# A buffer of its own for x, both halves per k-step, ten matmuls on zeros ahead of all, and later statistics in a decoder trunk on one NeuronCore

## The chip, the cores and the metric

The kernel runs on one core of a Trainium2 chip (trn2). The metric is the device time of one execution in microseconds (us). The profile is one execution, recorded by the hardware profiler. PE stands for TensorE's matmuls, PEld for its weight loads, DVE for VectorE, ACT for ScalarE, POOL for GpSimd, SP for SyncE, whose queue issues the large loads.

## What is computed

The reference is a small decoder trunk on 256 tokens of 1024 float32 channels. Two layers; each is a half-step FFN, a token mixer and another half-step FFN, each behind its own RMS norm:

```python
def rmsnorm(x, g):
    y = x * rsqrt(mean(x * x, axis=-1, keepdims=True) + 1e-6)
    return y * g

def swiglu_half_step(h, g, w1, w3, w2):
    u = rmsnorm(h, g)
    return h + 0.5 * ((silu(u @ w1) * (u @ w3)) @ w2)

h = x
h = swiglu_half_step(h, ...)                  # layer 0, FFN 0
h = h + mamba2_mixer(rmsnorm(h, ssm_norm), ...)
h = swiglu_half_step(h, ...)                  # layer 0, FFN 1
k_shared, v_shared = shared_kv(h, ...)
h = swiglu_half_step(h, ...)                  # layer 1, FFN 0
h = h + sliding_window_attention(rmsnorm(h, attn_norm), k_shared, v_shared, ...)
h = swiglu_half_step(h, ...)                  # layer 1, FFN 1
```

w1 and w3 are 1024 x 2816, w2 is 2816 x 1024. All of it is float32, and the weights are read once.

## The kernel before, in words

**Precision.** Each float32 operand is split into two parts of a faster type (float32r): a high part, made on ScalarE by a cast, and the remainder, made on VectorE by a subtraction. A product is then three matmuls (`wmm3`, L136): high x high, high x low, low x high. Almost all matmuls have 128 x 128 weights and 256 moving columns (the 256 tokens).

**Weights.** `Unit` (L142) takes a 1 MB piece of weights: a tile `raw` (three buffers, pool `rawp`), loaded by SyncE (L151), and for each 512 columns a cast `wh` on ScalarE (L164) and a subtraction `wl` on VectorE (L165). High and low parts have eight half-size buffers each, that is, four units. `up_unit` (L176) holds four of the eight k-tiles of 256 columns of w1 and w3; `row_unit` (L189) holds 256 rows of w2.

**FFN.** `run_ffn` (L294) goes through eleven chunks c of 256 hidden channels. For each chunk and each half f of 128 channels, `up(c, f)` (L330) makes w1's and w3's products in one PSUM bank `pm`: 2 x 8 k-tiles x 3 = 48 matmuls. `gate` (L315) makes silu(a) * b and splits it into `ghl`; `flush` (L363) adds the down product of a gated half into four PSUM banks `acc`: 24 matmuls. The first half of the first chunk runs k-tile by k-tile, with w1 and w3 in turn; all other halves run w1 over all k-tiles and then w3.

**The norm.** The up products of the first two chunks don't wait for the RMS norm: they use the hidden state times the gain, split into `vh` and `vl` (L242), and `gate` multiplies by the tokens' scale afterwards (L318). The later chunks use the normalized `uTh`, `uTl`, made by `normalize` (L282). The scale is made in steps: `square` (L249) squares the hidden state on ScalarE and adds the four parts on GpSimd (L255, L257); `stats` (L267) takes the mean with four small matmul instructions (`pc`), then VectorE and GpSimd make the reciprocal root `rs`; `scale` (L279) spreads it over partitions with matmuls (`pb`) and copies it to `rsb` (L222). When `stats` and `scale` are put into TensorE's stream is said by `at`: after so many matmuls of this FFN (`later`, L123, and `tick`, L126). It is (114, 134) for the first FFN and (60, 84) for the others. Where the second number is above 96 (`slow`, L392), the gates of chunk 0 and the normalize are put behind the third group of up products, not behind the second; in that case the first three flushes (72 down matmuls) follow the fourth group.

**The start.** x (1 MB) is loaded in two halves into `xin`, which takes one of the three raw buffers (L58); two weight units take the other two. `turn_x(b)` (L1110) transposes two of the eight k-tiles of x on TensorE, splits them into `vh`, `vl`, and splits the part of the weights that goes with them. b = 0 and 1 run ahead of the first FFN; 2 and 3 run inside the first half's k loop, at k = 3 and 5 (`pre`, L1135). `keep_x` (L1126), at k = 7, copies the transposed x from PSUM to `hT` on VectorE (L1129) and starts the squares. `gain_cols` (L198) transposes the gains.

**PSUM.** Three pools: `ps_mm` with two banks, `ps_acc` with four, `ps_tr` with two. The first half's `pm` is in `ps_acc`, the others are in `ps_mm`; the last two transposed pieces of x take two banks of `ps_acc`, and the four `acc` banks come from there as well.

**The order of work.** The framework orders each engine's instructions when the program is built: by the program's order as priority, and by a model of when inputs and buffers come free. Each engine then runs its list strictly in order. So matmuls of the second half may stand among those of the first, and a small load of a later stage may stand early in GpSimd's list: mamba's first tiles (L449 to L492) are filled in the first 10 us.

Of the kernel before, what the change touches and what calls it, by code (L numbers as in the profile page):

```python
# [11 lines left out]
F32 = mybir.dt.float32  # L12
# [6 lines left out]
P = 128  # L19
D = 1024  # L20
KT = D // P
S = 256
NT = S // P
# [17 lines left out]
def yoco_kernel(ctx: ExitStack, tc: tile.TileContext, a: dict, out: bass.AP):  # L41
    nc = tc.nc
# [3 lines left out]
    rawp = ctx.enter_context(tc.tile_pool(name="rawp", bufs=3))  # L46
# [3 lines left out]
    ps_mm = ctx.enter_context(tc.tile_pool(name="ps_mm", bufs=2, space=PSUM))  # L50
    ps_acc = ctx.enter_context(tc.tile_pool(name="ps_acc", bufs=4, space=PSUM))
# [3 lines left out]
        return bass.AP(tensor=src.tensor, offset=src.offset + off, ap=[[0, parts], [1, n]])  # L55

    x2 = a["x"][0]
    xin = rawp.tile([P, NT, D], F32, tag="raw", name="xin")  # L58
    xsrc = x2.rearrange("(t p) c -> p t c", p=P)
    nc.sync.dma_start(xin[:, :, 0:512], xsrc[:, :, 0:512])  # L60
    grow = [sb.tile([4 * KT, P], F32, tag="g", name="grow0", bufs=3),
# [23 lines left out]
    uTh = const.tile([P, KT, S], F32R, name="uTh")  # L85
    uTl = const.tile([P, KT, S], F32R, name="uTl")
# [3 lines left out]
    def nm(s):  # L90
        uid[0] += 1
        return f"{s}_{uid[0]}"
# [102 lines left out]

    gcols = []

    def gain_cols(g):  # L198
        n = g.shape[0]
        pg = ps_mm.tile([P, n], F32, tag="mm", name=nm("pg"))  # L200
        nc.tensor.transpose(pg, g, ident[:n, :n])
        gc = const.tile([P, n], F32, name=nm("gcol"))
        nc.scalar.copy(gc, pg)
        gcols.append(gc)
# [89 lines left out]
    def run_ffn(layer, j, cur, nxt, hook=None, ups=None, at=(60, 84), pre=None):  # L294
# [4 lines left out]
        ups = {} if ups is None else ups  # L299
# [15 lines left out]
        def gate(c, pm):  # L315
            if c < 2:
                t = sb.tile([P, 512], F32, tag="cv", name=nm("tp"), bufs=2)
                nc.vector.tensor_mul(half(t), half(pm), two(cur.rb))  # L318
                pm = t
            sl = sb.tile([P, 256], F32, tag="g", name=nm("sl"), bufs=3)  # L320
            nc.scalar.activation(sl, pm[:, 0:256], AF.Silu)  # L321
            g = sb.tile([P, 256], F32, tag="g", name=nm("g"), bufs=3)
            nc.vector.tensor_mul(g, pm[:, 256:512], sl)  # L323
            ghl = sb.tile([P, 512], F32R, tag="ghl", name=nm("ghl"), bufs=4)
            gh, gl = ghl[:, 0:256], ghl[:, 256:512]
            nc.scalar.copy(gh, g)
            nc.vector.tensor_sub(gl, g, gh.bitcast(F32))
            return gh, gl

        def up(c, f):  # L330
            u = units(c)
            xh, xl = (cur.vh, cur.vl) if c < 2 else (uTh, uTl)
            pool, tag = (ps_acc, "acc") if c == 0 and f == 0 else (ps_mm, "mm")
            pm = pool.tile([P, 512], F32, tag=tag, name=nm("pm"))

            def one(k, w, first, stop):
                wh, wl = u[k // 4].get((k % 4) * 512 + w * 256 + f * P, P)
                wmm3(pm[:, w * 256:(w + 1) * 256], wh, wl, xh[:, k, :], xl[:, k, :], first, stop)

            if c == 0 and f == 0:  # L340
                for k in range(KT):
                    if pre and k in pre:
                        pre[k]()
                    for w in range(2):
                        one(k, w, k == 0 and w == 0, k == KT - 1 and w == 1)
            else:
                for w in range(2):
                    for k in range(KT):
                        one(k, w, k == 0, k == KT - 1)
            return pm  # L350

        def down(c, f, d, g):
# [29 lines left out]

        pend = []

        def start_gates(pm):
            if hook is not None:
                cur.keep_eps()
            pend.append((0, 0, gate(0, g00)))
            pend.append((0, 1, gate(0, pm)))
            cur.normalize()  # L390

        slow = at[1] > 96  # L392
        for c in range(NCHUNK):
            for f in range(2):
                if c == 0 and f == 0:
                    later(*stats)
                    later(*scale)
                    with tc.issue_after(pe[-1]) if pe else nullcontext():
                        g00 = up(c, f)
                    continue  # L400
                pm = up(c, f)
                if c == 0 and not slow:
                    start_gates(pm)
                if c == 0:
                    g01 = pm
                    continue
                if slow and c == 1 and f == 0:
                    start_gates(g01)
# [493 lines left out]
    def attention(ap, cur, kT, vtok, bias, nxt):  # L902
# [199 lines left out]
    n0 = norms[0]  # L1102
    n0.open()
    w13 = a["ffn_w1"][0, 0], a["ffn_w3"][0, 0]
    ups = {0: [up_unit(*w13, 0, 0, 2, True,
                       lambda: nc.sync.dma_start(xin[:, :, 512:1024], xsrc[:, :, 512:1024]))]}
    ups[0].append(up_unit(*w13, 0, 1, 2, True))
# [18 lines left out]
    def keep_x():  # L1126
        for b, px in enumerate(pxs):
# [55 lines left out]
```

## Time and profile before

| what | value |
|---|---|
| median of 3 runs | 1079.51 us (1075.5 to 1083.77) |
| the profiled execution's own time | 1079.0 us |
| its span, first to last instruction | 1077.3 us |
| mean granted TensorE clock | 0.989 |
| loads from memory | 187.00 MB, 175 GB/s over the span |

The first FFN takes the stretch from the start to 206 us, mamba that to 413, the second FFN that to 604, the third that to 780; attention ends at 882 and the last FFN at the end.

How to read the rows: a row of a timeline has start, duration, engine, line, operation, what is written from what, shapes, count, and in brackets the engine's idle time before it and what ended that. A row of the chain of waits has start, duration, what. In a table of windows each engine has its busy time and, in brackets, the number of its instructions; then come the granted TensorE clock (1.00 is full), the mean share of the DMA engines and GB/s. A matmul's duration in a row is its latency; matmuls overlap, so what one costs is the distance from start to start.

### The profile page before, as it was taken

What the parts mean: (1) busy time and instruction counts of PE and PEld (TensorE: products, weight loads), DVE (VectorE), ACT (ScalarE), POOL (GpSimd) and SP (SyncE); (2) the same over time, 40 slices, a digit from 0 to 9 for tenths busy, and PEclk for the clock granted to TensorE, in tenths of its full rate; (3) what the DMA queues carried; (4) which work ended last, traced back from release to release, by engine and by line L of the source; (5) the groups of instructions that cost most, each with busy time, mean ns of one, the idle gap of its engine ahead of it and who ended that gap; (6) DMA issues with size and microseconds to landing.
All of it is one profiled execution on the core that took longest, in us unless ns stands there. A gap on an engine that the chain in (4) does not pass through costs nothing.

```text
span 1077.3 us, 20452 instructions
## 1 busy us (share of the span) xinstructions
PE 1049.3 (97%) x8262; PEld 1009.5 (94%) x8262; DVE 697.8 (65%) x1383; ACT 580.9 (54%) x1200; POOL 108.7 (10%) x104
## 2 busy tenths in 40 slices
PE   7999999999989989999999999999999999999998
PEld 6999999999879989999999999999997699999997
DVE  6955546784898877754555976555576769454543
ACT  5644545666876846553454755444565656353541
POOL 4000000103415123000000200010012010000000
PEclk9999999999989989999999999999999999999999
DMA  7566456548567345564656465665552326564641
GB/s 246 193 224 208 159 195 192 161 157 229 145 206 244 118 119 160 195 198 163 226 157 196 157 196 183 207 237 196 172 182 79 118 79 201 190 210 143 205 148 40
DMA packets 140944, 189.45 MB, mean 176 GB/s; under 512 B 4893, under 2 KB 120785, under 8 KB 140849
## 3 DMA queue, kind: packets, MB, share of 16 engines
q1 hardware_dynamic: 139632, 185.62, 53.4%
q0 software_dynamic: 1168, 2.51, 0.9%
q8 instruction: 65, 1.06, 0.4%
q14 instruction: 31, 0.25, 0.1%
q10 hardware_dynamic: 48, 0.02, 0.0%
HBM read 187.00 MB, written 1.12 MB: 175 GB/s over the span
## 4 chain that ended last, share of the span: by engine, by line
PE 85%; DVE 6%; ACT 3%; DMA 2%; issue 2%; POOL 1%; SPq 0%; ACTq 0%; DVEq 0%; POOLq 0%
PE pm L103 44%; PE acc L103 22%; PE pp L103 6%; PE pa L103 5%; PE pq L101 2%; DVE wl L165 2%; PE pa L101 1%; DMA raw<-in_ssm_w_in_dram 1%; POOL sq L255 1%; PE pz L103 1%; ACT wh L164 1%; DVE y L757 1%; PE ps L101 1%; PE po L101 1%; DVE sp L953 1%
## 5 line engine op out<-in xcount | busy, mean ns | idle before, releaser
L165 DVE TENSOR_TENSOR wl<-raw,wh 128x512 fp32r<-128x512 f32 x676 | 445.7, 707 | 148.9 <-ACT wh L164 147.7
L164 ACT CAST wh<-raw 128x512 fp32r<-128x512 f32 x676 | 378.8, 618 | 201.3 <-PE pm L103 100.7
L103 PE MATMUL pm<-uTh,wh 128*128 128x256 f32 x1152 | 323.4, 281 | 0.0
L103 PE MATMUL pm<-uTl,wh 128*128 128x256 f32 x1152 | 323.4, 281 | 0.0
L103 PE MATMUL pm<-uTh,wl 128*128 128x256 f32 x1152 | 323.3, 281 | 0.0
L103 PEld LDWEIGHTS pm<-uTh,wh 128*128 128x128 f32 x1152 | 217.2, 189 | 0.9 <-issue 0.2
L103 PEld LDWEIGHTS pm<-uTl,wh 128*128 128x128 f32 x1152 | 216.9, 188 | 0.6
L103 PEld LDWEIGHTS pm<-uTh,wl 128*128 128x128 f32 x1152 | 217.2, 189 | 0.0
L103 PE MATMUL acc<-ghl,wh 128*128 128x256 f32 x1056 | 190.6, 282 | 0.0
L103 PEld LDWEIGHTS acc<-ghl,wh 128*128 128x128 f32 x1056 | 162.3, 188 | 0.0
L103 PE MATMUL acc<-ghl,wl 128*128 128x256 f32 x528 | 148.8, 282 | 0.0
L323 DVE TENSOR_TENSOR g<-pm,sl 128x256 f32<-128x256 f32 x72 | 30.3, 421 | 135.8 <-ACT sl L321 135.8
L321 ACT ACTIVATE sl<-pm 128x256 f32<-128x256 f32 x72 | 27.3, 380 | 165.2 <-PE pm L103 165.2
L103 PEld LDWEIGHTS acc<-ghl,wl 128*128 128x128 f32 x528 | 99.5, 188 | 0.0
L103 PE MATMUL pp<-uTh,wl 128*128 128x256 f32 x288 | 82.9, 289 | 4.6 <-DVE wl L165 4.6
L103 PE MATMUL pp<-uTh,wh 128*128 128x256 f32 x288 | 83.4, 291 | 1.4 <-ACT uTh L291 1.4
L103 PE MATMUL pp<-uTl,wh 128*128 128x256 f32 x288 | 83.1, 290 | 0.2 <-DVE uTl L292 0.2
L255 POOL TENSOR_TENSOR sq<-sq,sq 128x512 f32<-128x512 f32 x18 | 27.8, 1544 | 519.0 <-ACT sq L251 519.0
L103 PE MATMUL pm<-vh,wl 128*128 128x256 f32 x256 | 74.3, 291 | 2.1 <-DVE wl L165 2.1
L103 PE MATMUL pm<-vh,wh 128*128 128x256 f32 x256 | 74.7, 292 | 0.5 <-DVE tp L318 0.3
L103 PE MATMUL pm<-vl,wh 128*128 128x256 f32 x256 | 73.9, 289 | 0.8 <-DVE vl L244 0.8
L103 PEld LDWEIGHTS pp<-uTh,wl 128*128 128x128 f32 x288 | 56.5, 196 | 4.8 <-DVE wl L165 4.8
(235 smaller groups left out, 1502.1 us busy)
## 6 DMA issues: line engine op xcount, KB each, us to landing
raw<-in_ffn_w_dram SPq DMA_DIRECT2D x172, 512.0 KB, 4.9
raw<-in_ffn_w_dram SPq DMA_DIRECT2D x44, 1024.0 KB, 5.3
raw<-in_ssm_w_in_dram SPq DMA_DIRECT2D x16, 1024.0 KB, 5.4
raw<-in_ssm_w_out_dram SPq DMA_DIRECT2D x8, 1024.0 KB, 4.9
em<-pdram SPq DMA_DIRECT2D x8, 768.0 KB, 11.0
raw<-in_ssm_w_in_dram SPq DMA_DIRECT2D x8, 512.0 KB, 4.8
raw<-in_w_q_dram SPq DMA_DIRECT2D x4, 1024.0 KB, 4.9
raw<-in_w_o_dram SPq DMA_DIRECT2D x4, 1024.0 KB, 5.0
```

Of the source, the lines that this page charges most:

```text
L101: r = op(*args, **kw)
L103: r = op(*args, **kw)
L164: return (nc.scalar.copy(wh, rs).ins, nc.vector.tensor_sub(wl, rs, wh.bitcast(F32)).ins)
L165: nc.vector.tensor_sub(wl, rs, wh.bitcast(F32)).ins)
L255: nc.gpsimd.tensor_add(self.sq, self.sq, sq)
L321: nc.scalar.activation(sl, pm[:, 0:256], AF.Silu)
L323: nc.vector.tensor_mul(g, pm[:, 256:512], sl)
L757: nc.vector.scalar_tensor_tensor(out=y2, in0=zs[:, j, :], scalar=gn(ct), in1=rb, op0=ALU.mult, op1=ALU.mult)
L953: chain[1] = op(*args, **kw).ins
```

## The change

- `xin` comes from a pool of its own, `xp`, with a 128 x 128 tile of zeros, `dummy`. The pool is closed behind the first FFN, so that mamba's pool takes over its memory.
- `keep_warm(10)` puts ten float32 matmuls of `dummy` by `dummy` (into a `ps_mm` bank that nobody reads) ahead of all other work of TensorE.
- `up_first` takes the place of the two halves of chunk 0, in all four FFNs: for each k-tile, both halves, and in each w1 and w3, so 12 matmuls per k-tile. In the first FFN both `pm` banks are in `ps_acc`.
- In the first FFN the third group, `up(1, 0)`, also runs k-tile by k-tile.
- In the first FFN `turn_x(2)`, `turn_x(3)` and `keep_x` run at k = 2, 4 and 7 of this longer loop, and `at` is (122, 143).
- In the second FFN (layer 0, FFN 1) `at` is (72, 95); in the other two it stays (60, 84).

```diff
     x2 = a["x"][0]
-    xin = rawp.tile([P, NT, D], F32, tag="raw", name="xin")
+    xpool = ExitStack()
+    xp = xpool.enter_context(tc.tile_pool(name="xp", bufs=1))
+    xin = xp.tile([P, NT, D], F32, name="xin")
+    dummy = xp.tile([P, P], F32, name="dummy")
+    nc.vector.memset(dummy, 0.0)
...
+    def keep_warm(n):
+        pw = ps_mm.tile([P, P], F32, tag="mm", name=nm("pw"))
+        for i in range(n):
+            nc.tensor.matmul(pw, dummy, dummy, start=True, stop=True)
+
...
+        def up_one(c, f, pm, k, w, first, stop):
+            xh, xl = (cur.vh, cur.vl) if c < 2 else (uTh, uTl)
+            wh, wl = units(c)[k // 4].get((k % 4) * 512 + w * 256 + f * P, P)
+            wmm3(pm[:, w * 256:(w + 1) * 256], wh, wl, xh[:, k, :], xl[:, k, :], first, stop)
+
+        def up_first():
+            pms = [ps_acc.tile([P, 512], F32, tag="acc", name=nm("pm")),
+                   (ps_acc if pre else ps_mm).tile([P, 512], F32, tag="acc" if pre else "mm", name=nm("pm"))]
+            for k in range(KT):
+                if pre and k in pre:
+                    pre[k]()
+                for f in range(2):
+                    for w in range(2):
+                        up_one(0, f, pms[f], k, w, k == 0 and w == 0, k == KT - 1 and w == 1)
+            return pms
+
         def up(c, f):
...
+            pm = ps_mm.tile([P, 512], F32, tag="mm", name=nm("pm"))
+            if c == 1 and f == 0 and pre:
                 for k in range(KT):
-                    if pre and k in pre:
-                        pre[k]()
                     for w in range(2):
-                        one(k, w, k == 0 and w == 0, k == KT - 1 and w == 1)
-            else:
-                for w in range(2):
-                    for k in range(KT):
-                        one(k, w, k == 0, k == KT - 1)
+                        up_one(c, f, pm, k, w, k == 0 and w == 0, k == KT - 1 and w == 1)
+                return pm
+            for w in range(2):
+                for k in range(KT):
+                    up_one(c, f, pm, k, w, k == 0, k == KT - 1)
             return pm
...
-        def start_gates(pm):
+        def start_gates():
             if hook is not None:
                 cur.keep_eps()
-            pend.append((0, 0, gate(0, g00)))
-            pend.append((0, 1, gate(0, pm)))
+            for f in range(2):
+                pend.append((0, f, gate(0, g0[f])))
             cur.normalize()
...
+    keep_warm(10)
...
-    run_ffn(0, 0, norms[0], norms[1], ups=ups, at=(114, 134),
-            pre={3: lambda: turn_x(2), 5: lambda: turn_x(3), 7: keep_x})
+    run_ffn(0, 0, norms[0], norms[1], ups=ups, at=(122, 143),
+            pre={2: lambda: turn_x(2), 4: lambda: turn_x(3), 7: keep_x})
+    xpool.close()
...
-        run_ffn(0, 1, norms[2], norms[3])
+        run_ffn(0, 1, norms[2], norms[3], at=(72, 95))
```

More of the change, by code (lines that the diff above doesn't have):

```diff
@@ L328, in gate @@
             return gh, gl
-        def up(c, f):
[L331 to L340, printed above, removed]
+        def up_one(c, f, pm, k, w, first, stop):
[12 more added lines that the diff above has]
+            return pms
+        def up(c, f):
+            pm = ps_mm.tile([P, 512], F32, tag="mm", name=nm("pm"))
+            if c == 1 and f == 0 and pre:
                 for k in range(KT):
-                    if pre and k in pre:
-                        pre[k]()
                     for w in range(2):
-                        one(k, w, k == 0 and w == 0, k == KT - 1 and w == 1)
-            else:
-                for w in range(2):
-                    for k in range(KT):
-                        one(k, w, k == 0, k == KT - 1)
+                        up_one(c, f, pm, k, w, k == 0 and w == 0, k == KT - 1 and w == 1)
[3 more added lines that the diff above has]
+                    up_one(c, f, pm, k, w, k == 0, k == KT - 1)
             return pm
@@ L398, in run_ffn @@
                     with tc.issue_after(pe[-1]) if pe else nullcontext():
-                        g00 = up(c, f)
+                        g0 = up_first()
+                    if not slow:
+                        start_gates()
+                if c == 0:
                     continue
                 pm = up(c, f)
[L402 to L406, printed above, removed]
                 if slow and c == 1 and f == 0:
-                    start_gates(g01)
+                    start_gates()
                 g = gate(c, pm)
```

## The prediction

> **What bounds the kernel now.** I read the page's busy shares first, then what TensorE waits for, then the chain of waits from the start to 50 us, then the timelines of TensorE, VectorE and GpSimd at the places where TensorE stood.
>
> ```profile
> PE 1049.3 (97%) x8262; PEld 1009.5 (94%) x8262; DVE 697.8 (65%) x1383; ACT 580.9 (54%) x1200; POOL 108.7 (10%) x104
> ```
>
> TensorE is busy 97% of a span of 1077.3 us. The change takes no matrix product out, so it can only win where TensorE stands still or runs slowly. TensorE's waits:
>
> ```profile
> PE px L1115 <- DMA xin<-in_x_dram: 5.5, 2, 5.3
> ...
> PE pm L103 <- DVE wl L165: 2.1, 2, 1.1
> PE pc L103 <- POOL sq L257: 1.9, 2, 1.7
> ```
>
> The columns are us in total, times, longest. All three are in the up-projections that the change touches (pc is the token mean of `stats`). The windows of the start (us, engines' busy time, granted clock, DMA share, GB/s) and single matmuls:
>
> ```profile
> 7.80:12.40 4.60, 4.28 (x19) 3.99 (x20) 3.33 (x8) 3.21 (x9) 1.61 (x3) 1.00 1.09 345
> 12.40:24.10 11.70, 11.70 (x98) 11.63 (x97) 10.22 (x17) 7.70 (x16) 2.16 (x2) 1.00 0.81 269
> 24.10:28.70 4.60, 2.26 (x13) 1.47 (x13) 4.54 (x5) 3.97 (x9) 3.28 (x3) 1.00 0.46 163
> ```
>
> ```profile
> 29.48:32.90 3.42, 3.42 (x18) 3.42 (x18) 2.35 (x4) 1.67 (x3) 1.11 (x1) 0.51 0.69 199
> ```
>
> ```profile
> 11.54 0.42 PE L103 MATMUL pm<-vl,wh 128*128 128x256 f32 x1
> 11.75 0.42 PE L103 MATMUL pm<-vh,wl 128*128 128x256 f32 x1
> ...
> 13.13 0.28 PE L103 MATMUL pm<-vh,wl 128*128 128x256 f32 x1
> 13.25 0.28 PE L103 MATMUL pm<-vh,wh 128*128 128x256 f32 x1
> ...
> 32.24 0.96 PE L103 MATMUL pb<-ident,rs 128*128 128x128 f32 x4
> 32.94 0.37 PE L103 MATMUL pm<-vh,wh 128*128 128x256 f32 x1
> ```
>
> Until about 12.4 us a matmul follows the last after 0.21 us, later after 0.12: a half-speed start, though the clock column still says 1.00 there. TensorE stands for half of 24.1 to 28.7, and soon after, from 29.48 to 32.90, the granted clock is 0.51. Why it stands is in the chain of waits:
>
> ```profile
> 14.20 5.16 DMA raw<-in_ffn_w_dram
> ...
> 19.96 1.16 ACT sq L251 x2
> ...
> 21.20 1.30 POOL sq L255
> ...
> 27.14 1.07 POOL sq L257
> ...
> 28.25 0.61 PE pc L103 x4
> ...
> 41.05 8.62 PE acc L103 x72
> ```
>
> The third weight unit starts loading at 14.20, once x has left the raw buffer; ScalarE's in-order queue holds a cast of it, with the squares behind it; the squares feed GpSimd's adds; the adds feed pc. VectorE in the same time:
>
> ```profile
> 7.36 0.48 DVE L244 SCALAR_TENSOR_TENSOR vl<-px,gcol,vh 128x256 fp32r<-128x256 f32 x1 [7.36 <-ACT vh L243]
> ...
> 17.11 2.48 DVE L1129 COPY hT<-px 128x512 f32<-128x512 f32 x4
> 20.09 0.69 DVE L165 TENSOR_TENSOR wl<-raw,wh 128x512 fp32r<-128x512 f32 x1 [0.51 <-ACT wh L164]
> 21.65 7.70 DVE L165 TENSOR_TENSOR wl<-raw,wh 128x512 fp32r<-128x512 f32 x7 [0.87 <-ACT wh L164]
> ...
> 29.34 2.48 DVE L165 TENSOR_TENSOR wl<-raw,wh 128x512 fp32r<-128x512 f32 x4
> 33.23 0.42 DVE L222 COPY rsb<-pb 128x256 f32<-128x256 f32 x1 [1.41 <-PE pb L103]
> ...
> 46.41 0.42 DVE L327 TENSOR_TENSOR ghl<-g,ghl 128x256 fp32r<-128x256 f32 x1
> ```
>
> From 17 us VectorE has almost no idle time: 0.51, 0.87 and 1.41 us. Seven splits of weights took 7.70, where four took 2.48 (0.62 each, so seven are 4.3): 3.4 us were lost while GpSimd added. So two engines bound the start together, and TensorE's idle time is not all to be won.
>
> **The change, part by part, at the start.** *x in its own pool.* No load is added; the third unit (1 MB) waits for no buffer and follows the second one directly. At 345 GB/s (the first window) 1 MB is 3.0 us, so it has landed by about 15.5, before ScalarE is through with the second unit, and the idle 0.51 and 0.87 on VectorE go. The squares no longer stand behind a cast without data: the first can run after the first copy (17.11 + 0.68), at 17.8 instead of 19.96. Then pc can come at 26.1 instead of 28.25. Eighteen matmuls lie between `stats` and `scale`, before and after (both marks move by 8 or 9): 2.2 us at full speed, so pb is through by 28.7 and rsb can start at 29.4, 3.8 us sooner. VectorE allows less: its splits of the third and fourth unit end at 29.35 - 1.38 = 27.97, four of the next unit (2.48) stand in the same queue, so rsb starts at 30.45, 2.8 us sooner. What follows rsb is VectorE's: from 33.23 to 46.83 (gates of chunk 0, normalize, gate of (1,0)) it ran 13.6 us with hardly a pause, and the third group of down matmuls (24 of the 72 in the acc row, from 46.6) needs that gate. I carry the 13.6 over unchanged. **The start so wins 2.8 to 3.8; I take 3.3.** Above that the next thing late would be this VectorE chain, which TensorE would reach 2 to 3 us early, however the matmuls before it are arranged.
>
> *The memory behind x.* mamba's pool takes over x's place after the pool closes, so mamba's early small loads must now wait for the last transpose of x:
>
> ```profile
> 4.05 0.21 POOL L450 MEMSET rows<- 128x128 f32 x1
> ...
> 8.49 0.92 POOL L490 DMA_DIRECT2D wdt<-in_ssm_w_in_dram  x1
> ```
>
> ```profile
> 34.47 0.27 PE L463 MATMUL ptc<-ident,rows 128*128 128x128 f32 x1
> ```
>
> These 5.4 us of GpSimd's in-order queue move from 4.05-9.41 to about 14.0-19.4 (the load at 14.20 waited for the same transposes). The adds, behind them in time, could begin at about 19.0 (two squares after 17.8): cost 0.4 at most if the queue is as said, up to 1.0 if an add is put behind a load that waits. TensorE reads the first of the small tiles only at 34.47. I take 0.
>
> *Both halves per k-step; the second chunk in k order too.* Instructions and count stay (192 matmuls to the first flush). Each unit is asked for half as fast (12 matmuls, 1.43 us, per k, against VectorE's about 1.0 for a split of x and one of weights). From 12.4 to 24.1 TensorE was already continuously busy, because the framework put the second half's matmuls in between; so at the start: 0. The second half's accumulator moves to the other PSUM pool, so the fourth up group no longer waits for a gate; it sits under the VectorE chain: 0.
>
> *Ten matmuls on zeros.* They need only a VectorE fill, and VectorE is idle until 7.36. An f32 matmul is two instructions; two of them (four instructions) took 32.94 - 32.24 = 0.70 at low clock, so ten take 3.5 us, from about 1.2 to 4.7, and x comes at 5.27 (the 5.3 of the wait): hidden. If they start 1 us later they cost 0.5. What they may win: the 15 or so projections of 7.9 to 12.4 at 0.12 instead of 0.21, 1.4 us of TensorE. But the projections are fed by VectorE's splits, and VectorE sets the pace all the way to 46.83: bounds 0 and 1.0; I take 0, being nearer to the engine that is full. The Trainium skill ("TensorE: Matmul & The Clock Gate", Part 1) says the clock is judged in free-running windows of 3.4 us and falls back after an idle one, which speaks against the ten: behind them comes a thin stretch of transposes. The trace agrees so far as the clock was 0.51 for 3.4 us behind the thin stretch before 28.7; by the rule the warm clock may be gone again by 9 us and the ten win nothing, by the row of the cold matmuls they could win the 1.0.
>
> **The later FFNs.** The second FFN also takes its statistics later (72 instead of 60, 95 instead of 84):
>
> ```profile
> 413.18 0.28 PE L103 MATMUL pm<-vh,wh 128*128 128x256 f32 x1
> ...
> 422.24 0.61 PE L103 MATMUL pc<-mean,sq 128*128 128x1 f32 x4 [1.72 <-POOL sq L257]
> ...
> 433.30 0.41 PE L103 MATMUL acc<-ghl,wh 128*128 128x256 f32 x2
> ```
>
> ```profile
> 416.79 4.59 POOL L255 TENSOR_TENSOR sq<-sq,sq 128x512 f32<-128x512 f32 x1 [2.69 <-ACT sq L251]
> 421.46 0.72 POOL L257 TENSOR_TENSOR sq<-sq 128x256 f32<-128x256 f32 x1
> ```
>
> ```profile
> 417.17 3.09 DVE L165 TENSOR_TENSOR wl<-raw,wh 128x512 fp32r<-128x512 f32 x5
> ...
> 431.76 0.42 DVE L327 TENSOR_TENSOR ghl<-g,ghl 128x256 fp32r<-128x256 f32 x1
> ```
>
> Twelve more matmuls before pc are 1.44 us of cover for a wait of 1.72: pc would be asked for at 413.18 + 72 x 0.12 = 421.8 and the adds end at 422.18. **Win 1.4.** The price could be at the first flush: the gate was ready at 432.18, 1.1 before 433.30, and pb comes 9 to 11 matmuls (1.1 to 1.3 us) nearer to it. Cover: the first unit's buffers are free after 48 matmuls, not 84, so the splits that stood ahead of that gate run earlier. I take 0; without it, 0.3.
>
> In the third FFN (default marks):
>
> ```profile
> 603.67 0.28 PE L103 MATMUL pm<-vh,wh 128*128 128x256 f32 x1
> ...
> 608.61 0.39 PE L103 MATMUL pm<-vl,wh 128*128 128x256 f32 x1 [0.34 <-DVE vl L244]
> ...
> 612.18 0.50 PE L103 MATMUL pc<-mean,sq 128*128 128x1 f32 x4
> ```
>
> Without waits pc would stand at 603.67 + 60 x 0.12 = 610.9; it lost 1.3 to waits for the last parts of v, of which the row shows the first. With 12 matmuls per k, k = 6 is asked for at 603.67 + 72 x 0.12 = 612.3, after both have come. But pc then comes 1.3 earlier itself and may meet the adds. **Win 1.0** (0 to 1.3). In the last FFN TensorE waits for nothing: 0.
>
> **Sum.** 3.3 + 1.4 + 1.0 = 5.7 off the profiled execution: 1079.0 (span 1077.3 and 1.7 around it) gives 1073.3. The median shown is 1079.51, 0.5 above it: **1073.8 us**. By the bounds of the terms (2.8 - 1.0 - 0.5 + 1.1 + 0 = 2.4, 3.8 + 1.0 + 1.7 + 1.3 = 7.8) it would be 1071.7 to 1077.1.
>
> **The rivals.**
> *TensorE alone bounds the start.* If the framework's new order puts the gate of (1,0) ahead of the normalize pieces, VectorE's chain falls away and the first flush follows pb by 48 matmuls: 28.7 + 5.8 = 34.5 instead of 41.05. Win 6.5 + 2.4 = 8.9: 1070.6. For it: TensorE is the engine named in the chain after pc. Against: VectorE's order followed the program, normalize before that gate.
> *The start's win is given back.* The adds of GpSimd now collide with copies and splits earlier; the 3.4 us lost to them may grow by the 2.8 that VectorE gains. Win only about 2: 1077.5. For it: the 4.59 us add.
> *The order isn't what was written.* The framework already mixed both halves at the start; if it undoes the k order in the later FFNs too, the third FFN's 1.0 and part of the 1.4 stay away: 1075.5.
> *Slower: GpSimd's adds are starved in the later FFNs.* The add of 4.59 us (its kind takes 1.3) ran beside five splits in a row and ended when they had. With unit 0 free after 48 matmuls, ScalarE and VectorE get up to eight more splits (8 x 0.62 = 5.0 us) before the adds are through. pc in the second FFN would wait until 422.18 + 5.0 = 427.2 against 421.8, 5.4 instead of 1.72; in the third the same 5.0 stands against 1.3; the last, without a wait now, could lose as much as 4. Together +3.7 + 3.7 + 4 - 3.3 = 8: 1087.5. It is slower from about three splits more per FFN. Against it: the next unit's load comes only after these splits, so they have no data. The Trainium skill ("SBUF — State Buffer", Who interferes with whom) says that a VectorE instruction with two SBUF inputs and a GpSimd one that reads SBUF lock each other out for one whole instruction; by it an add would wait for one split, 0.6, and this rival would be worth less than 2 us in all, but the row of 4.59 shows an add held by several.
>
> **How the numbers follow.** Forecast 0.48, TensorE alone 0.20, given back 0.20, order undone 0.06, starved 0.06. The single runs shown reach from 1075.5 to 1083.77, so 1% (10.8 us) is about what a measurement here tells from no change. Faster by more needs under 1068.7: only the first rival with a point more in each term or a new order in the mamba stage gets there, 0.10. Slower by more needs over 1090.3: the starved case at its worst, 0.03. Within 1%: 0.87. The range takes in the first two rivals and 3 us for the runs' own spread, without the starved case: 1067.5 to 1081.0.
>
> **What would show it.** Right: the third unit's load is issued before 5 us and there is no ScalarE wait for a load near 19; squares begin near 18; pc at 25.5 to 27; rsb at 29.4 to 30.5; TensorE stands 2 to 3 us before the third group of down matmuls, which begins at 43 to 44; in the second FFN pc waits under 0.5; in the third no wait for vl. Wrong: TensorE runs from pb into the flushes without standing (first rival); wl rows near 25 us longer than before (second); a pc wait over 2 us in a later FFN (starved). A mamba stage that changes its length by over 2 us would be something that I have not foreseen.

## The result and the profile after

| | median | runs |
|---|---|---|
| before | 1080.94 us | 1075.5 to 1083.77, 7 runs |
| after | 1088.53 us | 1086.33 to 1089.8, 7 runs |

After over before is 1.0074, 95% interval [1.0055, 1.0092]: slower by 7.6 us, where 5.7 us less was forecast. The profiled executions took 1079.0 and 1089.8 us (spans 1077.3 and 1088.1); the second is the slowest of its seven runs, so the profiles lie further apart than the medians. The first matmul of the stage that follows, from the timelines of TensorE, says where the 10.8 us of the spans lie (us). The third FFN of the kernel before ends at 799.93, not at the 780 that the section on the profile before gives.

| stage ends | before | after | stage longer by |
|---|---|---|---|
| first FFN (with the start) | 205.89 | 208.96 | 3.07 |
| mamba | 413.18 | 416.38 | 0.13 |
| second FFN | 603.67 | 609.29 | 2.42 |
| third FFN | 799.93 | 805.92 | 0.37 |
| attention | 882.23 | 888.37 | 0.15 |
| last FFN | 1077.3 | 1088.1 | 4.66 |

What TensorE waited for in the kernel after (total us, times, longest):

```profile
PE pc L107 <- POOL sq L266: 11.7, 3, 6.1
...
PE pw L205 <- DVE dummy L62: 1.1, 1, 1.1
PE pb L107 <- POOL rs L217: 1.0, 1, 1.0
```

Before, pc waited for GpSimd for 1.9 us in all. Now it is 11.7, in three places. They stand in TensorE's timeline of the kernel after, with the rows of the zeros and of the third FFN:

```profile
1.12 4.64 PE L205 MATMUL pw<-dummy 128*128 128x128 f32 x20 [1.12 <-DVE dummy L62]
5.54 0.66 PE L1129 MATMUL px<-ident,xin 128*128 128x128 f32 x4
...
7.67 0.39 PE L107 MATMUL pm<-vh,wh 128*128 128x256 f32 x1 [0.70 <-ACT wh L168]
...
10.65 0.28 PE L107 MATMUL pm<-vl,wh 128*128 128x256 f32 x1
10.77 0.28 PE L107 MATMUL pm<-vh,wl 128*128 128x256 f32 x1
...
30.15 1.01 PE L107 MATMUL pc<-mean,sq 128*128 128x1 f32 x4 [6.12 <-POOL sq L266]
...
34.59 1.05 PE L107 MATMUL pb<-ident,rs 128*128 128x128 f32 x4
...
427.81 0.61 PE L107 MATMUL pc<-mean,sq 128*128 128x1 f32 x4 [2.64 <-POOL sq L266]
...
616.49 0.50 PE L107 MATMUL pc<-mean,sq 128*128 128x1 f32 x4
...
898.62 0.61 PE L107 MATMUL pc<-mean,sq 128*128 128x1 f32 x4 [2.91 <-POOL sq L266]
...
900.27 0.42 PE L107 MATMUL pm<-vh,wl 128*128 128x256 f32 x1
900.48 0.41 PE L107 MATMUL pm<-vh,wh 128*128 128x256 f32 x1
```

TensorE stood 6.12 us at the start, 2.64 in the second FFN and 2.91 in the last. What held GpSimd is seen when its adds are laid beside VectorE's timeline. First GpSimd, kernel after:

```profile
19.16 0.92 POOL L503 DMA_DIRECT2D wdt<-in_ssm_w_in_dram  x1
21.53 3.74 POOL L264 TENSOR_TENSOR sq<-sq,sq 128x512 f32<-128x512 f32 x1 [1.44 <-ACT sq L260]
...
419.96 6.98 POOL L264 TENSOR_TENSOR sq<-sq,sq 128x512 f32<-128x512 f32 x1 [2.70 <-ACT sq L260]
...
891.99 5.78 POOL L264 TENSOR_TENSOR sq<-sq,sq 128x512 f32<-128x512 f32 x1 [2.70 <-ACT sq L260]
```

Then VectorE in the same kernel:

```profile
20.45 3.70 DVE L169 TENSOR_TENSOR wl<-raw,wh 128x512 fp32r<-128x512 f32 x6
...
419.54 0.87 DVE L253 SCALAR_TENSOR_TENSOR vl<-hT,gcol,vh 128x256 fp32r<-128x256 f32 x2
420.33 5.49 DVE L169 TENSOR_TENSOR wl<-raw,wh 128x512 fp32r<-128x512 f32 x9
...
892.35 4.30 DVE L169 TENSOR_TENSOR wl<-raw,wh 128x512 fp32r<-128x512 f32 x7
```

Each add ends 1.12 us after the last split of its row: 419.96 + 6.98 = 426.94 against 420.33 + 5.49 = 425.82; 897.77 against 896.65; 25.27 against 24.15. An add by itself took 1.29 us. So it did nearly all of its work only when the row of splits was over. In the second and the last FFN it waited through nine and seven of them; at the start it came during the second of six and waited through the rest. Before the change the row in the second FFN was five splits (the 3.09 us of the prediction, and again 1.12 us between the ends: 421.38 and 420.26).

The granted clock makes each stand dearer. Windows of the kernel after:

```profile
26.00:28.00 2.00, 0.00 (x0) 0.00 (x0) 1.35 (x1) 1.13 (x3) 1.27 (x1) 0.53 0.45 178
...
34.00:36.00 2.00, 2.00 (x11) 2.00 (x11) 0.32 (x1) 0.00 (x0) 0.00 (x0) 0.50 0.00 0
36.00:38.00 2.00, 2.00 (x17) 2.00 (x16) 2.00 (x5) 0.67 (x2) 0.00 (x0) 0.91 0.09 17
...
430.00:432.00 2.00, 2.00 (x12) 2.00 (x11) 0.00 (x0) 0.00 (x0) 0.00 (x0) 0.50 0.75 240
432.00:434.00 2.00, 2.00 (x17) 2.00 (x17) 0.96 (x2) 0.75 (x2) 0.00 (x0) 0.92 0.00 1
...
900.00:902.00 2.00, 2.00 (x12) 2.00 (x11) 0.83 (x3) 0.85 (x2) 0.59 (x1) 0.50 0.26 79
902.00:904.00 2.00, 2.00 (x14) 2.00 (x14) 1.09 (x2) 0.29 (x1) 0.00 (x0) 0.66 0.91 291
```

At 0.50 the matmuls start 0.21 us apart (900.27 and 900.48 above) instead of 0.12. In the second and the last FFN it lasts from about 429 to 432.4 and from 900 to 903.4: 16 matmuls each, 1.5 us lost each. In the second FFN 0.9 us more of waiting (2.64 for 1.72) and these 1.5 us are the whole 2.4. Before, neither stage had a half clock there (the windows of before from 422 to 430 and from 888 to 898 us show 1.00).

### The profile page after: what moved, and what is told of

It reads as the page before. It is cut to its first block, busy times and chain, and to the rows that moved or that the text cites. A ratio compares the mean times of both kernels' runs of the same rounds, so it can differ in the third digit from the quotient of the medians.

```text
span 1088.1 us, 20507 instructions
## 1 busy us (share of the span) xinstructions
PE 1055.1 (97%) x8282; PEld 1016.1 (93%) x8282; DVE 694.0 (64%) x1384; ACT 583.0 (54%) x1200; POOL 114.5 (11%) x104
## 3 DMA queue, kind: packets, MB, share of 16 engines
HBM read 187.00 MB, written 1.12 MB: 173 GB/s over the span
## 4 chain that ended last, share of the span: by engine, by line
PE 83%; DVE 6%; ACT 4%; POOL 3%; DMA 3%; issue 2%; SPq 0%; ACTq 0%; DVEq 0%; POOLq 0%
PE pm L107 43%; PE acc L107 22%; PE pp L107 6%; PE pa L107 4%; DVE wl L169 2%; POOL sq L264 2%; PE pq L105 2%; DMA raw<-in_ffn_w_dram 1%; ACT wh L168 1%; PE pa L105 1%; DMA raw<-in_ssm_w_in_dram 1%; PE pz L107 1%; DVE y L770 1%; PE ps L105 1%; PE po L105 1%
## 5 line engine op out<-in xcount | busy, mean ns | idle before, releaser
L169 DVE TENSOR_TENSOR wl<-raw,wh 128x512 fp32r<-128x512 f32 x676 | 441.0, 700 | 146.9 <-ACT wh L168 145.4
L264 POOL TENSOR_TENSOR sq<-sq,sq 128x512 f32<-128x512 f32 x18 | 36.2, 2012 | 510.1 <-ACT sq L260 510.1
```

Of the source, the lines that this page charges most:

```text
L169: nc.vector.tensor_sub(wl, rs, wh.bitcast(F32)).ins)
L264: nc.gpsimd.tensor_add(self.sq, self.sq, sq)
```

## The experiments

The ratio is to runs of the kernel before that were taken together with the kernel on the same chip. Their own medians lie between 1078.86 and 1080.94 us, so where two kernels were not taken together, the ratios compare them better than the medians.

| kernel | median us | ratio [95%] |
|---|---|---|
| after, adds on VectorE | 1071.46 | 0.9919 [0.9903, 0.9935] |
| after, later FFNs in the old order | 1081.74 | 1.0024 [1.0008, 1.004] |
| after, no zeros | 1084.69 | 1.0039 [1.002, 1.0059] |
| before, x in its own pool | 1081.76 | 1.0016 [1.0002, 1.003] |
| before, adds on VectorE | 1073.82 | 0.9942 [0.9921, 0.9962] |
| after, adds on VectorE, later FFNs in the old order | 1073.29 | 0.9942 [0.9922, 0.9962] |
| after, adds on VectorE, squares ahead | 1072.45 | 0.9929 [0.9908, 0.995] |
| after, adds on VectorE, gate ahead | 1072.75 | 0.9931 [0.991, 0.9952] |
| after, last add on VectorE | 1075.64 | 0.9963 [0.9943, 0.9983] |
| after, adds on VectorE, no zeros | 1076.24 | 0.9956 [0.9941, 0.9971] |
| after, adds on VectorE, squares and gate ahead | 1072.97 | 0.9926 [0.99, 0.9952] |
| before, adds on VectorE, zeros | 1073.34 | 0.9947 [0.9926, 0.9968] |

**Is it the adds on GpSimd?** The theory (A): VectorE's splits keep the adds waiting, longer than before because more of them follow each other. The rival (B): TensorE only asks for pc too early. The adds of squares and the fold move to VectorE:

```diff
-            nc.gpsimd.tensor_add(self.sq, self.sq, sq)
+            nc.vector.tensor_add(self.sq, self.sq, sq)
...
-                nc.gpsimd.tensor_add(self.sq[:, 0:S], self.sq[:, 0:S], self.sq[:, S:2 * S])
+                nc.vector.tensor_add(self.sq[:, 0:S], self.sq[:, 0:S], self.sq[:, S:2 * S])
```

> The changed kernel with one thing moved: the adds of the squares run on VectorE instead of GpSimd. Theory A (GpSimd's adds are kept waiting by VectorE's splits in a row, of which the change makes more): the waits for pc (6.1, 2.6 and 2.9 us in the changed kernel's profile) go nearly to 0, the half-clock stretches behind them go too, and the time falls by 8 to 13 us, to 1076 to 1080 us. Theory B (TensorE asks for pc too early, whoever adds; the squares themselves come late): the waits stay above half of what they are, and since VectorE has 18 more adds of 0.7 us to do, the time stays at 1085 us or more.

1071.46 us (1069.68 to 1075.22), 17.1 less than after, and more than the 8 to 13 that theory A gave. Its profile is of its slowest execution, and even there no pc waits for GpSimd. VectorE in the second FFN, this kernel:

```profile
415.23 0.69 DVE L264 TENSOR_TENSOR sq<-sq,sq 128x512 f32<-128x512 f32 x1
415.83 0.68 DVE L169 TENSOR_TENSOR wl<-raw,wh 128x512 fp32r<-128x512 f32 x1
416.43 0.42 DVE L266 TENSOR_TENSOR sq<-sq 128x256 f32<-128x256 f32 x1
416.76 4.90 DVE L169 TENSOR_TENSOR wl<-raw,wh 128x512 fp32r<-128x512 f32 x8
```

The add takes 0.69 us at its place in the queue, and the eight splits come behind it, not beside it. TensorE still asks for pc as early as in the kernel after (8.6 us after the second FFN's first matmul). So A's mechanism holds, and B falls.

**How much of it is the last add?** Only the third add of each norm and the fold move:

```diff
-            nc.gpsimd.tensor_add(self.sq, self.sq, sq)
+            (nc.vector if b == 3 else nc.gpsimd).tensor_add(self.sq, self.sq, sq)
```

(and the fold as above)

> The kernel after with only the last of the three adds of squares and the fold behind it on VectorE; the first two adds stay on GpSimd. Theory A (the loss is the last add of each norm, which stands on GpSimd beside a row of VectorE's splits that the change made longer): nearly all of the gain of the kernel with all adds on VectorE comes, 1071 to 1075 us, and no wait of TensorE for GpSimd above 0.5 us at pc in the second and the last FFN. At the start the first add may still be held (3.7 us beside six splits in the kernel after), so pc there 28 to 30 us. Rival (the early adds count as well, each norm's two adds on GpSimd are late too): 1077 to 1083 us, with pc waits of 1 us or more in the later FFNs.

1075.64 us (1074.24 to 1078.58): 12.9 of the 17.1 us. That is a little above the theory's numbers; of the rival's waits of 1 us or more for GpSimd there is none in the list of waits. The early adds at the start, this kernel, GpSimd:

```profile
21.10 1.84 POOL L264 TENSOR_TENSOR sq<-sq,sq 128x512 f32<-128x512 f32 x1 [0.35 <-ACT sq L260]
23.68 1.56 POOL L264 TENSOR_TENSOR sq<-sq,sq 128x512 f32<-128x512 f32 x1 [0.74 <-ACT sq L260]
```

They were not held through a row in this execution, and pc came at 27.74. In others the first may be, as in the kernel after; that could be the remaining 4 us, but no profile shows it.

**Is it the same in the kernel before?** The adds move to VectorE there (the same two lines):

> The kernel before with the adds of the squares on VectorE and nothing else. Theory A (the lock is what both kernels lose by; the change only made it worse): the kernel before also gets faster, by the 1.7 us wait in the second FFN, by as much in the executions where the last FFN's add is kept waiting too, and by up to 3.4 us at the start: 1074 to 1077 us, some 3 to 5 us above the changed kernel with the same adds (1071.5), which is what the change itself is worth once the lock is gone. Rival: the change is worth nothing of itself, and all the gain is that of the adds: 1071 to 1072 us.

1073.82 us (1069.68 to 1075.92), 6.4 less than the 1080.26 of the runs of before beside it: just under theory A's numbers and above the rival's. So the adds on GpSimd cost the kernel before as well. With the adds on VectorE, the change's own worth is 1073.82 - 1071.46 = 2.4 us, but the intervals of the two ratios overlap: not told apart from nothing. By the profiles the FFNs two to four are as long in both (188.5, 195.0, and 195.6 against 195.1), and the first ends at 205.52 against 205.22.

**The order in the later FFNs.** The kernel after, with the old loops and the old marks in all FFNs but the first:

```diff
-        run_ffn(0, 1, norms[2], norms[3], at=(72, 95))
+        run_ffn(0, 1, norms[2], norms[3])
```

with `up_first` running, without `pre`, the first half over k and then w, and the second half over w and then k.

> The changed kernel with the first FFN as changed, and the three later FFNs in the order and with the marks of before (first half k by k, second half w1 then w3; (60, 84)). Theory A: the second FFN loses again the 2.5 us and the last one the 4.6 us by which they got longer, since fewer splits are ready during the adds; the third gives back up to 1.3; in all 1082 to 1084 us, and the start alone stays 3 us longer than before. Theory B: the marks of 60 in the second FFN are earlier than 72, so its wait for pc is no shorter than the 2.6 us of the changed kernel; in all 1085 us or more.

1081.74 us (1079.57 to 1087.71), just under theory A's numbers. By the ratios (1.0024 against 1.0074) two thirds of the loss come back; the rest would be the start, which this kernel shares with the kernel after, but in its profile the first FFN ends only 0.35 us later than before's, so that is not shown. In its profile the second FFN and the last both have an add of 4.6 us beside five splits, as the second had before, and pc waits 1.68 and 1.70. The last FFN, GpSimd, then VectorE:

```profile
885.12 4.58 POOL L264 TENSOR_TENSOR sq<-sq,sq 128x512 f32<-128x512 f32 x1 [2.69 <-ACT sq L260]
```

```profile
885.49 3.08 DVE L169 TENSOR_TENSOR wl<-raw,wh 128x512 fp32r<-128x512 f32 x5
```

So the row of splits is longer because of the order: with both halves per k, unit 0 is free after 48 matmuls. In the second FFN the edit takes back the marks as well; in the last FFN the order alone differs. With the adds on VectorE the same edit can't be told from nothing:

> The changed kernel with the adds on VectorE, and the later FFNs in the old order with the old marks. Theory A: without the lock the new order in the later FFNs wins what I predicted for the third (1.0 to 1.3, the waits for vl) and little in the second, which has no wait left to cover: 1072 to 1074 us. Rival: the new order wins nothing or costs: 1069 to 1071.5 us.

1073.29 us (1071.0 to 1076.47), beside 1071.46: inside theory A's numbers, but the intervals of the ratios overlap. What is shown is that the new order doesn't cost without the adds on GpSimd.

**The ten zero matmuls.** Left out of the kernel after:

```diff
-    keep_warm(10)
```

> The changed kernel without the ten matmuls on zeros. Theory A: TensorE reached the wait for pc 6.1 us early, so the slow clock of the first 5 us of work only shortens that wait: time within 1 us of the changed kernel's 1088.5, pc at about 30. Rival: the clock early on is worth its 1.4 us on the path, or more where the transposes of x come later and VectorE's start with them: 1090 to 1091.

1084.69 us (1077.87 to 1087.63), 3.8 less than after, a number that neither theory had. Twelve runs spread over 10 us, and the profile is of the fastest. It shows two things by which a run can be fast. The first is in the second FFN, GpSimd:

```profile
412.43 1.61 POOL L264 TENSOR_TENSOR sq<-sq,sq 128x512 f32<-128x512 f32 x1 [2.69 <-ACT sq L260]
```

and VectorE:

```profile
412.02 0.87 DVE L253 SCALAR_TENSOR_TENSOR vl<-hT,gcol,vh 128x256 fp32r<-128x256 f32 x2
412.81 7.15 DVE L169 TENSOR_TENSOR wl<-raw,wh 128x512 fp32r<-128x512 f32 x9
```

The same add meets the same nine splits as in the kernel after; it starts 0.38 us ahead of them (there 0.37), while the second of the same two vl runs. But here the add got in behind the vl: it ends at 414.04, 1.15 us after them, and the nine splits take 7.15 instead of 5.49. One side loses 1.66 us, or the other 5.7. That won 3.9 of the 11.9 us by which this span is shorter than that of the kernel after. The second thing is worth more, 5.1 us, and doesn't come from this add: it is in mamba. The windows of mamba, kernel after and this one:

```profile
208.96:416.38 207.42, 195.12 (x1596) 189.92 (x1595) 166.94 (x324) 139.63 (x278) 54.57 (x44) 0.96 0.58 172
206.50:408.86 202.36, 190.11 (x1596) 184.69 (x1595) 166.61 (x324) 139.06 (x278) 55.49 (x44) 0.98 0.59 176
```

The granted clock stood at 0.50 there for 17.1 us in the kernel after and for 6.8 here, and half of the difference, which is what the half clock costs, is 5.1. In its last FFN, this kernel's add was held all the same: 5.79 us, and pc waited 2.90.

The kernel before has the good outcome of the add too, in its last FFN. GpSimd, then VectorE, of before:

```profile
885.85 1.60 POOL L255 TENSOR_TENSOR sq<-sq,sq 128x512 f32<-128x512 f32 x1 [2.69 <-ACT sq L251]
```

```profile
886.22 4.74 DVE L165 TENSOR_TENSOR wl<-raw,wh 128x512 fp32r<-128x512 f32 x5
```

Five splits in 4.74 instead of 3.09: 1.65 lost. That is why TensorE waited for nothing there, and why the prediction put 0 for the last FFN: it read a won race as the rule. Of the ten such adds of the second and the last FFN in five profiles (before, after, after with the old order in the later FFNs, after without zeros, before with x in its own pool), these two alone got in early.

Where no add is on GpSimd, leaving out the zeros has the other sign:

> The kernel after with all adds on VectorE and without the ten zero matmuls, so that the zeros are priced where no add is held. Theory 1 (the zeros warm the clock 4.5 us earlier, but VectorE's chain to the gate of the third group absorbs that): 1071 to 1073 us, within 1 us of the 1071.5 of the kernel with the zeros; matmuls from 8 to 12.4 us at 0.21 apart, the third group of down matmuls at 45 to 46 us against 44.98. Rival (the 1.4 us of TensorE come through to the end): 1073 to 1075 us. Rival of the other sign (they cost): under 1070.5 us.

1076.24 us (1073.67 to 1078.1); the ratio's interval lies above that of the kernel with zeros. Both numbers of theory 1 and of the rival were too low: the zeros are worth some 4 us there. Their first part shows in the profiles: pc comes at 29.48 us without zeros against 27.69 with them, and the first FFN ends at 207.27 against 205.52. The rest isn't shown, since this profile is of the fastest of its runs. In the kernel before, the zeros do nothing that can be measured:

> The kernel before with all adds of squares on VectorE and the ten zero matmuls ahead of everything; x still in the raw buffer, both old loops, old marks. Without an add on GpSimd, leaving the zeros out of the changed kernel moved its median from 1071.46 to 1076.24 us. Theory 1 (the zeros are worth about 4 us by themselves, and the rest of the change then costs about 2): 1069 to 1071.5 us. Rival (the zeros pay only where x has its own buffer and the third unit's load needn't wait; here the warm matmuls meet weights that come late): 1073 to 1075 us, like the kernel before with the adds on VectorE alone (1073.82). Both show matmuls 0.12 us apart from the first projections on.

1073.34 us (1071.85 to 1074.93) against 1073.82: the rival. They do warm the clock there (projections 0.12 us apart in its timeline from 8.3 us on), but the first flush comes only 0.5 us sooner (39.70 against 40.23). So the zeros pay together with x's own buffer and the new first loop, and not by themselves.

**The start.** x in its own pool, alone, in the kernel before:

```diff
-    xin = rawp.tile([P, NT, D], F32, tag="raw", name="xin")
+    xpool = ExitStack()
+    xp = xpool.enter_context(tc.tile_pool(name="xp", bufs=1))
+    xin = xp.tile([P, NT, D], F32, name="xin")
```

> The kernel before with one part of the change: x in a pool of its own (no zero tile, old order, old marks). My prediction: squares begin near 18 us, pc near 26, the start is 2.8 to 3.8 us shorter, 1077 to 1078 us. Rival: the load that ScalarE's queue waits for is only another one (the fourth unit's instead of the third's), the squares stay behind it at 19.5 to 20.5, and the start gains less than 1 us: 1080 to 1082 us.

1081.76 us (1078.1 to 1085.82): no gain, the rival's number. ScalarE in this kernel:

```profile
16.50 2.81 ACT L166 CAST wh<-raw 128x512 fp32r<-128x512 f32 x5
19.21 1.15 ACT L253 ACTIVATE sq<-hT 128x512 f32<-128x512 f32 x2
```

The third unit's data did come early, so ScalarE had five casts to do ahead of the squares, which began 0.75 us sooner than in before, not 2.1; the first add then took 1.82 us, and pc came at 28.02 against 28.25. So the squares stood behind casts at work, not behind a cast that waited, as the rival had it.

Two more edits of the start stand on the kernel with the adds on VectorE. The casts of the fourth unit behind the second square on ScalarE:

```diff
-                ups[c] = [up_unit(w1, w3, c, 0), up_unit(w1, w3, c, 1)]
+                ups[c] = [up_unit(w1, w3, c, 0)]
+                with behind(*(sqi[1:2] if pre and c == 1 else ())):
+                    ups[c].append(up_unit(w1, w3, c, 1))
```

`sqi` lists the squares, and `behind` puts what it encloses after the second of them.

> The changed kernel with the adds on VectorE, and the casts of the fourth weight unit put behind the second square in ScalarE's list, so that no square stands behind a cast that waits for a load. Theory A (as in my prediction, the squares then begin at 18.5 to 19 instead of 20.3 and pc comes 1 to 1.5 earlier): rsb earlier by 1, the third group of down matmuls as well, 1069 to 1071 us. Rival: VectorE's own chain (splits, copies, adds) sets pc, and the casts that come later only delay it: 1071 to 1074 us.

1072.45 us (1069.95 to 1074.61): nothing to tell from 1071.46. The squares began at 19.60 instead of 20.81, yet pc came at 27.71 against 27.69, as the rival had it. The other puts the third group's gate ahead of the normalize pieces:

```diff
-            cur.normalize()
+            if not slow:
+                cur.normalize()
...
                 g = gate(c, pm)
+                if slow and c == 1 and f == 0:
+                    cur.normalize()
```

> The changed kernel with the adds on VectorE, and in the first FFN the gate of the third up group ahead of the normalize, not behind it. Theory A (VectorE's chain of 13.6 us from rsb to that gate bounds the start, and TensorE's pause of 2 us ahead of the third group of down matmuls then costs 1.8 us more at half clock): the pause goes, no half clock at 45 to 49 us, 3 to 4 us less: 1067 to 1069 us. Rival: the normalize pieces are then late by as much, the pause moves to the group after it: within 1 us of 1071.5.

1072.75 us (1070.05 to 1074.69), above theory A's numbers. The first FFN ends at 202.04 instead of 205.52 in the profile, and no half clock is left in it, yet the median doesn't move. Both together:

> The kernel after with all adds on VectorE, the casts of the fourth unit behind the second square on ScalarE, and the gate of the third group ahead of the normalize pieces. If the two edits each give what their profiles showed and add up: 1068 to 1070.5 us, first FFN through at 201 to 202 us against 205.5. Rival (TensorE is full: an earlier start is given back as waits for weights in the same FFN or later): 1071 to 1074 us, like each edit alone (1072.45 and 1072.75).

1072.97 us (1070.93 to 1074.15): the rival's number. In the profiles the first FFN ends at 201.24, 4.3 us sooner, and half of it is gone at the end: mamba takes 207.97 instead of 206.56, the third FFN 0.4 more, the last 0.3 more (spans 1071.3 and 1073.5). The list of waits of this kernel says of one product of mamba:

```profile
PE pp L107 <- DVE wl L169: 4.8, 1, 4.8
```

It was 4.1 in the kernel with the adds on VectorE alone, so part of it is a wait for weights. But mamba's length goes from 202.36 to 207.97 us over the fourteen profiles, so one profile of each kernel doesn't show that the earlier start is the reason; that TensorE is full is not shown. The fastest of all twelve by the median is the kernel with the adds on VectorE, 1071.46 us, 8.2 below the 1079.67 of the runs of before beside it; the others with all adds on VectorE are not told apart from it, except the one without zeros.

## Why the prediction was wrong

**The step that failed** is the one that put the new order of the later FFNs at nothing: "Cover: the first unit's buffers are free after 48 matmuls, not 84, so the splits that stood ahead of that gate run earlier. I take 0". That they run earlier was right, and it is the cost: they run beside the add. The rival *starved* had this, and was given 0.06 for the reason that "the next unit's load comes only after these splits, so they have no data". The rows of seven and nine splits without a pause, where there had been five, show that four and two more did have it.

Two more steps failed. At the start, the largest single term (-3.3, measured +3.1), the squares were taken to be free of any cast without data, and the longer hold of the first add was left to the rival *given back*. And no term of the sum held the half clock that followed a stand of TensorE, although the prediction showed such a stretch (0.51 for 3.4 us).

Point by point:
- *Second FFN, -1.4.* TensorE asked for pc 8.8 us after the stage's first matmul (427.81 - 2.64 - 416.38), as the prediction's 8.6 said. But the fold (the addition of the two halves, which ends the adds) ended 11.4 us after it, not 9.0. Measured: +2.4.
- *Third FFN, -1.0.* The waits for vl went and pc came 7.2 us after the first matmul, as worked out. The time went into the next step: pb waited 1.0 for rs, since VectorE made the small `me` only at 619.63, behind five splits and a piece of the hook, the shared key and value work that this FFN carries. Its adds were not held (1.42 and 1.36 us). Measured: +0.4.
- *Last FFN, 0.* Measured +4.7: 2.9 of waiting for pc and 1.5 of half clock; 0.2 is not followed. With the old order and the add held, this FFN took 197.3 against 195.07 of before (the profile of the kernel with the old order in the later FFNs), so about half of the 4.7 is the race that the profile of before had won.
- *Start, -3.3.* Measured +3.1 at the end of the first FFN, in one chain (kernel after, start, duration, what):

```profile
12.38 7.30 DMA raw<-in_ffn_w_dram
...
20.30 1.16 ACT sq L260 x2
...
21.53 3.75 POOL sq L264
...
26.01 1.27 POOL sq L264
...
29.37 0.74 POOL sq L266
...
30.15 1.01 PE pc L107 x4
```

The prediction had the squares at 17.8 since the third unit's load is early. It is; but then a cast of the *fourth* unit stands in ScalarE's queue, and its load took from 12.38 to 19.68. The squares came at 20.30, later than before (19.96). Then the first add was held by the row of six splits. pc came at 30.15 instead of 26.1, and the clock fell to 0.50 until 36 us. With the adds on VectorE the rest of the step came some 1 us later than it was worked out: rsb at 31.38, the third group of down matmuls at 44.98, 13.6 later, with TensorE standing 2.0 us before it. But then this stand brought the half clock in its turn, which the sum had left out. TensorE, then a window, of the kernel with the adds on VectorE:

```profile
43.67 0.35 PE L107 MATMUL pm<-uTh,wh 128*128 128x256 f32 x1 [1.97 <-DVE tp L327]
...
44.98 0.89 PE L107 MATMUL acc<-ghl,wh 128*128 128x256 f32 x5 [0.30 <-ACT ghl L335]
```

```profile
45.00:50.00 5.00, 5.00 (x29) 5.00 (x30) 5.00 (x11) 0.66 (x2) 0.00 (x0) 0.66 0.68 220
```

A mean of 0.66 over 5 us is 3.4 us at 0.50.
- *Both halves per k at the start, 0; GpSimd's moved loads, 0.* Right: TensorE ran without a pause until 24.0 us, and the loads ended at 20.1, before the squares were there.
- *Ten zero matmuls, 0 to 1.0.* They ran from 1.12 to 5.5 us and were hidden, and the first projections came 0.12 apart. The clock did not fall back in the thin stretch behind them, as the Trainium skill ("TensorE: Matmul & The Clock Gate", Part 1) let one fear. The size was off: some 4 us where no add is held.

The *starved* rival's 1087.5 is near the 1088.5 by way of other terms: it had +3.7 in the third FFN, where nothing was held, and a won start.

Kernels without a single add on GpSimd still spread by 3 to 6 us, and the time goes with the granted clock. The fastest run of the kernel with the adds on VectorE took 1069.68 us at a mean clock of 0.994, its slowest 1075.22 at 0.989; 0.005 of the time is an estimated 5.4 us, and the difference is 5.5. In the profiles mamba shows it: it took 202.36 and 203.07 us in the two with 6.8 us at 0.50 there, and 206.56 to 207.97 in the three with 20.5. So a difference of a few us between two profiles can come from there.

What stays open: why one execution has more of these stretches than another, and where the last 2 us of the zeros' worth lie.

## What to carry to other kernels

Before splits or copies on VectorE are pulled forward, look at what GpSimd does at that time on a path that TensorE waits for: a two-input GpSimd instruction can stand through the whole row, so its price is the length of the row, and it grows when buffers come free sooner. An elementwise step of 1.3 us on GpSimd that ends a chain may be cheaper as 0.7 us on the busy VectorE. A stage that shows no wait in one profile may have won a race: compare the same instruction in all layers before putting 0.

## What the runs showed of the hardware

- An add on GpSimd that starts while VectorE reads two SBUF operands got its turn either right behind that instruction (1.60 and 1.61 us in all, the splits then 1.65 and 1.66 longer) or only behind the last of the row: 4.59 us at five splits, 5.78 at seven, 6.98 at nine, each 1.12 after the last. At the same offset, 0.37 to 0.38 us, both happened. The Trainium skill ("SBUF — State Buffer", Who interferes with whom) says that the one who issues first has the ports for its whole instruction; by the rows, the one who waits can go without its turn through nine instructions in a row. The rows show the times, not the ports.
- Whether the outcome also differs between executions of one program is not shown, since each kernel has one profile. The twelve runs of the kernel without zeros lie between 1077.87 and 1087.63 us, but their granted clock differs too (0.993 in the two fastest, 0.984 to 0.989 in the others).
- Stands of TensorE of 2.0 us (the kernel with the adds on VectorE), 2.6 and 2.9 us were each followed by the clock at 0.50 for 3.4 us; in the 6.1 us stand it fell soon after 26 us, 2 us in, and stayed until about 36. The length of the stand alone doesn't decide: of five stands of about 1.7 us in the second and the last FFN (before; after with the old order in the later FFNs; before with x in its own pool) one was followed by such a stretch, from 892.5 us on in the last of these kernels, and a stand of 2.8 us in mamba was not (to 279.14 us, the kernel with the adds on VectorE and without zeros).
